# Step sizes of a state-space layer from the plain input, in four column groups of the array

## The chip, the cores and the metric

The kernel runs on one core of a Trainium2 chip. It is a single program in which five engines (PE for matrix products, DVE for elementwise work, ACT for activations and copies, POOL, and SP, which issues the transfers) each follow their own list of instructions and wait for one another through semaphores. The metric is the device time of one execution in microseconds, as the median of several runs.

## The reference: what is computed

One layer of a hybrid decoder is evaluated for a prompt of 1024 tokens and for eight short samples of 4 tokens, together 1056 columns. What matters here is the beginning of the layer:

```python
h = rmsnorm(x, norm_mix)
proj = h @ w_in
z, xbc, dt_raw, v_pool = jnp.split(proj, [D_SSM, D_SSM + D_XBC, D_SSM + D_XBC + SSM_HEADS], axis=-1)
xbc, conv_new = causal_dwconv(conv_buf, xbc, ssm_conv_w, ssm_conv_b)
xbc = jax.nn.silu(xbc)
...
dt = jax.nn.softplus((dt_raw + ssm_dt_bias).astype(f32))
a = -jnp.exp(ssm_a_log.astype(f32))
y, ssm_new = ssd_chunked(xs, dt, a, ...)
```

`dt_raw` is the projection of the normalized input onto 16 columns, one for each head of the recurrence: its step sizes. From them follow the decays, exp of running sums of `dt * a` in chunks of 128 tokens, which the recurrence needs. All is float32.

## The kernel before

Everything lies transposed: 128 channels on the partitions, the 1056 tokens along the free axis, as three blocks of 352 (`NB`, `BW`). The input x is eight such tiles, `xs[0..7]`. To reach float32 accuracy at the fast rate, most products are made in three passes from numbers split into a high and a low part of type float32r: weight high by input high, high by low, low by high. `x_split` makes `hh[k]` and `hl[k]` from `xs[k]` times the gain `norm_mix`. The factor of the norm (one for each token) is not known then; it is applied to the results afterwards, by `normed`, from the tile `rbc`.

**Foreground.** `mm_full` makes one tile of 128 output channels: eight steps over the input tiles, each with 9 matmuls of 352 columns, and after each step one call of `tick()`. The first two tiles are made together by `two_tiles` (16 ticks). A third follows, then the step sizes, then nine more tiles of the convolved part (`XBC_ORDER`), then 16 of gate and pooling (`VZ`), the output product of the pooling half (8 tiles), and the memory's K and V. The tiles' results stand in `pmm`, two buffers of three PSUM banks each, which the tiles take in turn; a tile can begin when the one before the last has been evicted. Two further banks (`mstile`) serve all small products. Weights come in half tiles through three buffers each of raw, high and low parts: ACT writes the high part (`wh`), DVE the low one (`wl`), two halves ahead of their use.

**Ticks.** `later(n, fn)` runs `fn` at the n-th tick from there. `background(gen, every)` puts a generator in a queue and runs a step of its head each `every` ticks. In this queue follow one another: the fold (`fold_pool`, which multiplies two weight matrices, 24 matmuls of 512 columns for each of four groups, 40 yields in all and a 41st call that ends it), the recurrence (`ssd_all`), its sample part (`ssd_sample`) and the gate (`gate_all`, 45 calls, what is left of it being run at the end of the K and V stage). A scheduler orders the instructions of each engine within the bounds of what is declared here; a flag (`strict`) keeps the written order in the beginning of the program.

**The steps that the change touches,** by the lines of the program before:

- `x_sq` (L513), at ticks 8 to 15: ACT squares `xs[k]` in place, DVE adds it into `xs[0]`. `norm_cols` at tick 18 sums over channels by PE transposes and DVE reductions and makes the factors; `x_bc` (L520) at tick 24 spreads them into `rbc` by further PE transposes (`ms<-cst,nr`).
- `dt_weights` (L526) at tick 10: ACT and DVE split the 16 weight columns into high and low, side by side as 32 columns.
- Behind the third tile, the step sizes (L706 to L712): for each of eight input tiles the 32 weight columns against `hh[k]` and `hl[k]`, 48 matmuls of 352 columns in all, into one 3-bank buffer, with a tick after each of the eight. While these run, the fold's first group is put between them. DVE applies the norm's factors (L713, L714).
- `dt_chain` (L534), six ticks later: nine PE transposes bring the step sizes' 32 rows onto token partitions, DVE adds the two halves and the bias, ACT and DVE make softplus by exp and a polynomial, four PE products (with `U`, ones, and two small masks) make the running sums and totals, and ACT makes the decays. The running sums go to DRAM (`scr_acs`), from where the recurrence loads them.

Of the kernel before, what the change touches and what calls it, by code (L numbers as in the profile page):

```python
# [39 lines left out]
SSD_AHEAD = 4  # L40
SAMPLE_EVERY = 1.5
GATE_EVERY = 1.5
FOLD_EVERY = 1.2
WINDOWS = (2, 4, 8, 16)
AHEAD = 2
UP_AHEAD = 5
# [34 lines left out]
def body(ctx, tc, A):  # L81
# [71 lines left out]
    def mmtile():  # L153
        return pmm[0].tile([P, NB, 512], F32, tag="mm", name="mm")
# [220 lines left out]
    def v3(t):  # L375
        return t[:, :T].rearrange("p (b n) -> p b n", b=NB)
# [59 lines left out]
    def bc_cols(r, w, out):  # L436
        c = 0
        while c * P < w:
            ps = mstile()
            c0 = c  # L440
            wsum = 0
            while c < c0 + 4 and c * P < w:
                wc = min(P, w - c * P)
                PE.transpose(ps[:, wsum:wsum + wc], r[:wc, c:c + 1].to_broadcast([wc, P]), ident[:wc, :wc])
                wsum += wc
                c += 1
            V.tensor_copy(out[:, c0 * P:c0 * P + wsum], ps[:, :wsum])
# [63 lines left out]
            prep()  # L511

    def x_sq(k):  # L513
        S.activation(xs[k][:, :T], xs[k][:, :T], AF.Square)
        if k:
            V.tensor_tensor(xs[0][:, :T], xs[0][:, :T], xs[k][:, :T], op=ALU.add)

    xr = []

    def x_bc():  # L520
        xr.append(lp.tile([P, T], F32, tag="rbc", name="rbc", bufs=1))
        bc_cols(xr[0], T, xr[1])

    wd = stile(F32R)[:, :256].rearrange("p (k s h) -> p k s h", k=KT, s=2)

    def dt_weights():  # L526
        wdv = wdr[:, :128].rearrange("p (k h) -> p k h", k=KT)
        S.activation(wd[:, :, 0], wdv, AF.Copy)
        V.tensor_tensor(wd[:, :, 1], wdv, wd[:, :, 0].bitcast(F32), op=ALU.subtract)

    def normed(out, ps):
        V.tensor_tensor(v3(out), ps[:, :, :BW], v3(xr[1]), op=ALU.mult)

    def dt_chain():  # L534
        ps = mstile()
        H2 = 2 * H
        for c in range(8):
            PE.transpose(ps[:, c * H2:(c + 1) * H2], dtr[:H2, c * P:(c + 1) * P], ident[:H2, :H2])
        V.tensor_copy(dtr[:H2, T:T + 2 * TS].rearrange("h (r t) -> h r t", r=2),
                      dtr[:H2, TP:T].unsqueeze(1).to_broadcast([H2, 2, TS]))  # L540
        PE.transpose(ps[:R3, 8 * H2:9 * H2], dtr[:H2, TP:TP + R3], ident[:H2, :H2])
        w = ttile()
        ws = [w[:, i * 144:(i + 1) * 144] for i in range(8)]
        x, u, s, s2, pl, da, ea = ws[:7]

        def v9(a):
            return a.rearrange("p (c h) -> p c h", c=9)

        V.memset(x, 0.0)
        psv = ps[:, :9 * H2].rearrange("p (c s h) -> p c s h", c=9, s=2)  # L550
        dtb = pc("dtb", 0, 16)
        V.tensor_tensor(v9(x)[:, :8], psv[:, :8, 0], dtb.unsqueeze(1).to_broadcast([P, 8, H]), op=ALU.add)
        V.tensor_tensor(v9(x)[:R3, 8], psv[:R3, 8, 0], dtb[:R3], op=ALU.add)
        V.tensor_tensor(v9(x)[:, :8], psv[:, :8, 1], v9(x)[:, :8], op=ALU.add)
        V.tensor_tensor(v9(x)[:R3, 8], psv[:R3, 8, 1], v9(x)[:R3, 8], op=ALU.add)
        V.scalar_tensor_tensor(u, x, -1.0, x, op0=ALU.mult, op1=ALU.min)
        S.activation(u, u, AF.Exp)
        V.tensor_scalar(s, u, 2.0, None, op0=ALU.add)
        V.reciprocal(s, s)
        V.tensor_tensor(s, s, u, op=ALU.mult)  # L560
        V.tensor_tensor(s2, s, s, op=ALU.mult)
        V.tensor_scalar(pl, s2, 1.0 / 15, None, op0=ALU.mult)
        for n in (13, 11, 9, 7, 5, 3):
            V.scalar_tensor_tensor(pl, pl, 1.0 / n, s2, op0=ALU.add, op1=ALU.mult)
        V.scalar_tensor_tensor(pl, pl, 1.0, s, op0=ALU.add, op1=ALU.mult)
        V.tensor_scalar(x, x, 0.0, None, op0=ALU.max)
        dtf = dt_t.rearrange("p c h -> p (c h)")
# [12 lines left out]
        V.tensor_copy(acs_t[:, :8], ps2[:, 0:128].rearrange("p (c h) -> p c h", c=8))  # L580
        V.tensor_copy(acs_t[:R3, 8], ps2[:R3, 256:272])
        V.tensor_tensor(de_t[:, :8], ps2[:, 128:256].rearrange("p (c h) -> p c h", c=8), acs_t[:, :8],
                        op=ALU.subtract)
        V.tensor_tensor(de_t[:R3, 8], ps2[:R3, 272:288], acs_t[:R3, 8], op=ALU.subtract)
        S.activation(cd_t[:, :8], ps2[:, 128:256].rearrange("p (c h) -> p c h", c=8), AF.Exp)
        S.activation(de_t, de_t, AF.Exp)
        V.tensor_tensor(de_t, de_t, dt_t, op=ALU.mult)
        at = ttile()
        for q in range(3):
            ps3 = mstile()  # L590
            n = min(4, 9 - 4 * q)
# [27 lines left out]
    def xbc_raw(f, ps=None):  # L619
        ps = ps or mm_full(KT, hh, hl)  # L620
        raw = ttile()
        if xr[1:]:
            normed(raw[:, 3:3 + T], ps)
        else:
            S.activation(v3(raw[:, 3:3 + T]), ps[:, :, :BW], AF.Copy)
        return raw
# [62 lines left out]
    for k in range(8):  # L689
        later(8 + k, lambda k=k: x_sq(k))  # L690
    later(10, dt_weights)
    later(XN_TICK, lambda: xr.append(norm_cols(xs[0], T, D)))
    later(XN_TICK + XN_LAG, x_bc)
    early_raw = [xbc_raw(f, ps) for f, ps in zip(XBC_ORDER[:2], two_tiles())]
    strict[0] = "after"
    background(fold_pool(), FOLD_EVERY)
    ps = mm_full(KT, hh, hl)
    for f, raw in zip(XBC_ORDER, early_raw):
        V.tensor_tensor(raw[:, 3:3 + T], raw[:, 3:3 + T], xr[1][:, :T], op=ALU.mult)
        xbc_conv(f, raw)  # L700
    raw = ttile()
    normed(raw[:, 3:3 + T], ps)
    xbc_conv(XBC_ORDER[2], raw)

    ps = mmtile()
    for k in range(KT):  # L706
        for pi, x in enumerate((hh[k], hl[k])):
            for b in range(NB):
                PE.matmul(ps[:2 * H, b, :BW], lhsT=wd[:, k].rearrange("p s h -> p (s h)"),
                          rhs=x[:, b * BW:(b + 1) * BW], start=(k == 0 and pi == 0), stop=(k == KT - 1 and pi == 1))  # L710
        tick()
    dtr = ttile()  # L712
    V.tensor_tensor(v3(dtr)[:2 * H], ps[:2 * H, :, :BW], v3(xr[1])[:2 * H], op=ALU.mult)  # L713
    later(6, dt_chain)  # L714
    strict[0] = False
    for f in XBC_ORDER[3:6]:
        xbc_tile(f)
# [217 lines left out]
    def pool_tile(f):  # L935
# [2 lines left out]
        G.memset(raw[:, 0:15], 0.0)  # L938
        ext = raw[:, 1039:1191].rearrange("p (b t) -> p b t", b=8)
        dma(ext[:, :, 0:15], A["pool_hist"][f])  # L940
        rb = v3(xr[1])
        V.tensor_tensor(raw[:, 15:719].rearrange("p (b n) -> p b n", b=2), ps[:, 0:2, :BW], rb[:, 0:2], op=ALU.mult)
        V.tensor_tensor(raw[:, 719:1039], ps[:, 2, :320], rb[:, 2, :320], op=ALU.mult)
        V.tensor_tensor(ext[:, :, 15:19], ps[:, 2, 320:352].rearrange("p (b t) -> p b t", b=8),
# [1081 lines left out]
```

## Time and profile before

| What | Value |
|---|---|
| median of three runs | 1649.13 us (1647.32 to 1649.66) |
| the profiled execution | 1645.04 us |
| its span, first to last instruction | 1642.9 us |
| PE, weight loads, DVE, ACT busy | 1624.7, 1553.6, 1214.1, 806.9 us |
| granted TensorE clock, mean | 0.999 |
| mean busy share of the DMA engines, 36 to 60 us | 0.25 |

All operations of the program go through one helper, so every row names line 93; they are told apart by tiles. `mm` is a 3-bank buffer, `ms` a small PSUM buffer, `s`, `t` and `ld` are working tiles of the kernel, `wh` and `wl` the split weights. In the rows, `mm<-s 128*32 128x352` is a matmul with 128 rows and 32 columns of weights, which streams 352 columns. Matmuls overlap in the records (one of 352 columns is shown with 0.32 us, and the next begins 0.16 after it), so their cost is read from start to start.

### The profile page before, as it was taken

To read this page: it belongs to the slowest core of one execution; us is meant where nothing else is said; L and a number is where in the kernel's file an instruction comes from. 1 tells how busy PE (TensorE), PEld (TensorE's weight loads), DVE (VectorE), ACT (ScalarE), POOL (GpSimd) and SP (SyncE) were. 2 spreads that over 40 slices of the span, in tenths; PEclk is the share of its full clock that TensorE was granted. 3 is DMA by queue.
4 is the path that set the end of the run, shared out by engine and by line. 5 is a ranking of instruction groups with operands and counts; after the bars stand their busy time and mean duration, and the time that the engine had idled before them with its cause. 6 is when DMAs were issued, how large, how long until landed. Compare 5 with 4: busy or idle time off the path is not lost.

```text
span 1642.9 us, 30318 instructions
## 1 busy us (share of the span) xinstructions
PE 1624.7 (99%) x11802; PEld 1553.6 (95%) x11802; DVE 1214.1 (74%) x2044; ACT 806.9 (49%) x1580; POOL 54.2 (3%) x117
## 2 busy tenths in 40 slices
PE   9999999999999999999999999999999999999998
PEld 8899999999989999999888999999999999999997
DVE  7766787788679676654654898888888998766665
ACT  7566643543505343223543665666665556554441
POOL 0110000001000000000000000000000000000000
PEclk9999999999999999999999999999999999999999
DMA  6244354544687688953755654544344356985542
GB/s 224 86 156 97 69 112 105 117 90 118 220 304 253 210 271 296 301 184 91 253 199 189 220 179 133 163 133 144 108 126 159 120 174 208 315 287 181 167 131 106
DMA packets 172286, 287.40 MB, mean 175 GB/s; under 512 B 39680, under 2 KB 77408, under 8 KB 172144
## 3 DMA queue, kind: packets, MB, share of 16 engines
q1 hardware_dynamic: 169280, 281.02, 54.3%
q0 software_dynamic: 2864, 4.46, 1.9%
q8 instruction: 92, 1.51, 0.4%
q14 instruction: 50, 0.41, 0.1%
HBM read 207.89 MB, written 77.53 MB: 174 GB/s over the span
## 4 chain that ended last, share of the span: by engine, by line
PE 89%; DMA 5%; DVE 4%; ACT 1%; issue 1%; SPq 0%; ACTq 0%; DVEq 0%
PE mb L93 60%; PE mm L93 22%; PE ms L93 6%; DVE s L93 2%; DMA q<-scr_g 2%; DVE wl L93 1%; ACT s L93 1%; DMA ld<-scr_pool 1%; DVE t L93 0%; DMA s<-xT 0%; SPq L93 0%; DMA ld<-scr_acs 0%; DMA t<-scr_z 0%; DMA ld<-h0T 0%; DMA wr<-scr_dn 0%
## 5 line engine op out<-in xcount | busy, mean ns | idle before, releaser
L93 PE MATMUL mb<-s,wh 128*128 128x264 f32 (+4 forms) x4800 | 901.5, 294 | 2.9 <-ACT wh L93 2.9
L93 PEld LDWEIGHTS mb<-s,wh 128*128 128x128 f32 x4800 | 756.6, 188 | 9.2 <-ACT wh L93 3.6
L93 PE MATMUL mb<-s,wl 128*128 128x264 f32 (+4 forms) x2400 | 663.4, 294 | 2.4 <-DVE wl L93 2.4
L93 PEld LDWEIGHTS mb<-s,wl 128*128 128x128 f32 x2400 | 445.0, 188 | 7.2 <-DVE wl L93 4.3
L93 ACT ACTIVATE wh<-wr 128x512 fp32r<-128x512 f32 (+1 forms) x266 | 164.2, 618 | 365.6 <-PE mb L93 170.1
L93 PE MATMUL mm<-s,wh 128*128 128x352 f32 x1728 | 340.3, 330 | 2.3 <-ACT s L93 1.3
L93 PEld LDWEIGHTS mm<-s,wh 128*128 128x128 f32 x1728 | 284.6, 188 | 8.5 <-ACT s L93 2.7
L93 DVE TENSOR_TENSOR wl<-wr,wh 128x512 fp32r<-128x512 f32 (+1 forms) x266 | 178.8, 673 | 103.0 <-ACT wh L93 101.4
L93 PE MATMUL mm<-s,wl 128*128 128x352 f32 x864 | 187.4, 323 | 0.0
L93 DVE SCALAR_TENSOR_TENSOR t<-t,par 128x1104 f32<-128x1104 f32 (+1 forms) x124 | 168.6, 1364 | 18.1 <-ACT t L93 17.3
L93 PEld LDWEIGHTS mm<-s,wl 128*128 128x128 f32 x864 | 147.2, 189 | 1.7 <-issue 1.2
L93 DVE TENSOR_TENSOR t<-t 128x1024 f32<-128x1024 f32 (+10 forms) x147 | 105.4, 729 | 8.2 <-DMA t<-w_dn 4.9
L93 ACT ACTIVATE wh<-ws 128x512 fp32r<-128x512 f32 x110 | 69.0, 628 | 71.0 <-PE mb L93 69.0
L93 DVE TENSOR_TENSOR wl<-ws,wh 128x512 fp32r<-128x512 f32 x110 | 75.6, 687 | 22.5 <-ACT wh L93 17.0
L93 DVE TENSOR_TENSOR s<-mb,s 128x264 f32<-128x264 f32 (+6 forms) x140 | 60.9, 472 | 30.3 <-PE mb L93 15.1
L93 ACT ACTIVATE t<-mb 128x264 f32<-128x264 f32 (+1 forms) x136 | 53.5, 394 | 57.9 <-PE mb L93 51.0
L93 ACT ACTIVATE s<-s 128x512 f32<-128x512 f32 (+7 forms) x87 | 65.1, 764 | 31.4 <-DMA s<-scr_acs 21.7
L93 DVE TENSOR_TENSOR s<-q,s 128x528 fp32r<-128x528 f32 x81 | 56.1, 703 | 24.3 <-ACT s L93 24.0
L93 ACT ACTIVATE t<-t,par 128x1104 f32<-128x1104 f32 (+1 forms) x56 | 73.0, 1304 | 1.5 <-DVE t L93 0.6
L93 ACT ACTIVATE s<-q 128x528 fp32r<-128x528 f32 x81 | 51.7, 643 | 41.2 <-DMA q<-scr_g 39.1
L93 DVE TENSOR_TENSOR s<-s 128x528 fp32r<-128x528 f32 (+8 forms) x76 | 64.5, 867 | 6.8 <-ACT s L93 6.3
L93 PE MATMUL mb<-s 128*128 128x256 f32 (+2 forms) x414 | 68.9, 323 | 0.0
(202 smaller groups left out, 1496.5 us busy)
## 6 DMA issues: line engine op xcount, KB each, us to landing
q<-scr_g SPq DMA_DIRECT2D x77, 264.0 KB, 3.7
wr<-w_up SPq DMA_DIRECT2D x59, 256.0 KB, 2.9
wr<-w_in SPq DMA_DIRECT2D x56, 256.0 KB, 3.2
wr<-w_mo SPq DMA_DIRECT2D x46, 256.0 KB, 2.8
scr_g<-t SPq DMA_DIRECT2D x22, 528.0 KB, 2.7
ws<-w_up SPq DMA_DIRECT2D x44, 256.0 KB, 2.9
t<-w_dn SPq DMA_DIRECT2D x32, 256.0 KB, 4.3
scr_dn<-t SPq DMA_DIRECT2D x32, 256.0 KB, 2.9
```

The source lines that it names most:

```text
L93: i = fn(*args, **kwargs)
```

## The change

1. The step sizes are made from plain x, not from the split input. The weight columns are multiplied by the gain `norm_mix` (DVE) and padded with zeros from 16 to 32 columns. Input tiles k = 0 to 3, and then 4 to 7, go to the four groups of 32 output partitions of one buffer: each group sums two of the eight input tiles. These are 24 plain float32 matmuls of 352 columns. They stand between the first two tiles and the third, without ticks. ACT copies the result, 128 rows, out of PSUM.
2. x must stay until then, so the squares go to other tiles and their sum to a tile of its own.
3. `dt_chain` applies the norm's factors, and instead of transposing multiplies each 128 tokens (as the weights) by `sel`, a 128 by 16 matrix of zeros and ones that adds up the four groups (the padded columns meet no one). These are nine plain float32 matmuls with 16 moving columns. Two of DVE's four additions behind them go.
4. The fold's steps come each 1.05 ticks instead of 1.2, and `dt_chain` ten ticks after the third tile, instead of six after the old place of the step sizes.

```diff
-FOLD_EVERY = 1.2
+FOLD_EVERY = 1.05
...
     def x_sq(k):
-        S.activation(xs[k][:, :T], xs[k][:, :T], AF.Square)
-        if k:
-            V.tensor_tensor(xs[0][:, :T], xs[0][:, :T], xs[k][:, :T], op=ALU.add)
+        if k == 0:
+            xr.append(stile())
+            S.activation(xr[0][:, :T], xs[0][:, :T], AF.Square)
+        else:
+            t = ttile()
+            S.activation(t[:, :T], xs[k][:, :T], AF.Square)
+            V.tensor_tensor(xr[0][:, :T], xr[0][:, :T], t[:, :T], op=ALU.add)
...
-    wd = stile(F32R)[:, :256].rearrange("p (k s h) -> p k s h", k=KT, s=2)
+    wd = stile()[:, :256].rearrange("p (k h) -> p k h", k=KT)
+    sel = xa.tile([P, H], F32, name="sel")
+    dtr3 = xa.tile([P, R3], F32, name="dtr3")
+    dtr = stile()
 
     def dt_weights():
-        wdv = wdr[:, :128].rearrange("p (k h) -> p k h", k=KT)
-        S.activation(wd[:, :, 0], wdv, AF.Copy)
-        V.tensor_tensor(wd[:, :, 1], wdv, wd[:, :, 0].bitcast(F32), op=ALU.subtract)
+        V.memset(wd, 0.0)
+        V.tensor_tensor(wd[:, :, :H], wdr[:, :128].rearrange("p (k h) -> p k h", k=KT),
+                        pc("norm_mix", 0, 8).unsqueeze(2).to_broadcast([P, KT, H]), op=ALU.mult)
+        V.tensor_reduce(sel, ident.rearrange("p (i h) -> p h i", h=H), axis=AX.X, op=ALU.add)
+
+    def dt_raw():
+        ps = mmtile()
+        for k in range(0, KT, 4):
+            for b in range(NB):
+                for j in range(4):
+                    PE.matmul(ps[32 * j:32 * j + 32, b, :BW], lhsT=wd[:, k + j],
+                              rhs=xs[k + j][:, b * BW:(b + 1) * BW], start=(k == 0), stop=(k == 4))
+        S.activation(v3(dtr), ps[:, :, :BW], AF.Copy)
...
     def dt_chain():
+        V.tensor_tensor(dtr[:, :T], dtr[:, :T], xr[2][:, :T], op=ALU.mult)
+        V.tensor_copy(dtr3.rearrange("h (r t) -> h r t", r=3), dtr[:, TP:T].unsqueeze(1).to_broadcast([P, 3, TS]))
         ps = mstile()
-        H2 = 2 * H
-        for c in range(8):
-            PE.transpose(ps[:, c * H2:(c + 1) * H2], dtr[:H2, c * P:(c + 1) * P], ident[:H2, :H2])
-        V.tensor_copy(dtr[:H2, T:T + 2 * TS].rearrange("h (r t) -> h r t", r=2),
-                      dtr[:H2, TP:T].unsqueeze(1).to_broadcast([H2, 2, TS]))
-        PE.transpose(ps[:R3, 8 * H2:9 * H2], dtr[:H2, TP:TP + R3], ident[:H2, :H2])
+        for c in range(9):
+            x = dtr[:, c * P:(c + 1) * P] if c < 8 else dtr3
+            PE.matmul(ps[:P if c < 8 else R3, c * H:(c + 1) * H], lhsT=x, rhs=sel, start=True, stop=True)
...
     early_raw = [xbc_raw(f, ps) for f, ps in zip(XBC_ORDER[:2], two_tiles())]
+    dt_raw()
     strict[0] = "after"
     background(fold_pool(), FOLD_EVERY)
     ps = mm_full(KT, hh, hl)
...
-    ps = mmtile()
-    for k in range(KT):
-        for pi, x in enumerate((hh[k], hl[k])):
-            for b in range(NB):
-                PE.matmul(ps[:2 * H, b, :BW], lhsT=wd[:, k].rearrange("p s h -> p (s h)"),
-                          rhs=x[:, b * BW:(b + 1) * BW], start=(k == 0 and pi == 0), stop=(k == KT - 1 and pi == 1))
-        tick()
-    dtr = ttile()
-    V.tensor_tensor(v3(dtr)[:2 * H], ps[:2 * H, :, :BW], v3(xr[1])[:2 * H], op=ALU.mult)
-    later(6, dt_chain)
+    later(10, dt_chain)
```

More of the change, by code (lines that the diff above doesn't have):

```diff
@@ L521, in x_bc @@
         xr.append(lp.tile([P, T], F32, tag="rbc", name="rbc", bufs=1))
-        bc_cols(xr[0], T, xr[1])
-    wd = stile(F32R)[:, :256].rearrange("p (k s h) -> p k s h", k=KT, s=2)
-    def dt_weights():
-        wdv = wdr[:, :128].rearrange("p (k h) -> p k h", k=KT)
-        S.activation(wd[:, :, 0], wdv, AF.Copy)
-        V.tensor_tensor(wd[:, :, 1], wdv, wd[:, :, 0].bitcast(F32), op=ALU.subtract)
+        bc_cols(xr[1], T, xr[2])
+    wd = stile()[:, :256].rearrange("p (k h) -> p k h", k=KT)
+    sel = xa.tile([P, H], F32, name="sel")
+    dtr3 = xa.tile([P, R3], F32, name="dtr3")
+    dtr = stile()
+    def dt_weights():
+        V.memset(wd, 0.0)
[10 more added lines that the diff above has]
+        S.activation(v3(dtr), ps[:, :, :BW], AF.Copy)
     def normed(out, ps):
-        V.tensor_tensor(v3(out), ps[:, :, :BW], v3(xr[1]), op=ALU.mult)
+        V.tensor_tensor(v3(out), ps[:, :, :BW], v3(xr[2]), op=ALU.mult)
     def dt_chain():
+        V.tensor_tensor(dtr[:, :T], dtr[:, :T], xr[2][:, :T], op=ALU.mult)
+        V.tensor_copy(dtr3.rearrange("h (r t) -> h r t", r=3), dtr[:, TP:T].unsqueeze(1).to_broadcast([P, 3, TS]))
         ps = mstile()
-        H2 = 2 * H
-        for c in range(8):
-            PE.transpose(ps[:, c * H2:(c + 1) * H2], dtr[:H2, c * P:(c + 1) * P], ident[:H2, :H2])
-        V.tensor_copy(dtr[:H2, T:T + 2 * TS].rearrange("h (r t) -> h r t", r=2),
-                      dtr[:H2, TP:T].unsqueeze(1).to_broadcast([H2, 2, TS]))
-        PE.transpose(ps[:R3, 8 * H2:9 * H2], dtr[:H2, TP:TP + R3], ident[:H2, :H2])
+        for c in range(9):
+            x = dtr[:, c * P:(c + 1) * P] if c < 8 else dtr3
+            PE.matmul(ps[:P if c < 8 else R3, c * H:(c + 1) * H], lhsT=x, rhs=sel, start=True, stop=True)
         w = ttile()
@@ L549, in dt_chain @@
         V.memset(x, 0.0)
-        psv = ps[:, :9 * H2].rearrange("p (c s h) -> p c s h", c=9, s=2)
+        psv = ps[:, :9 * H].rearrange("p (c h) -> p c h", c=9)
         dtb = pc("dtb", 0, 16)
[L552 to L555, printed above, removed]
+        V.tensor_tensor(v9(x)[:, :8], psv[:, :8], dtb.unsqueeze(1).to_broadcast([P, 8, H]), op=ALU.add)
+        V.tensor_tensor(v9(x)[:R3, 8], psv[:R3, 8], dtb[:R3], op=ALU.add)
         V.scalar_tensor_tensor(u, x, -1.0, x, op0=ALU.mult, op1=ALU.min)
@@ L621, in xbc_raw @@
         raw = ttile()
-        if xr[1:]:
+        if xr[2:]:
             normed(raw[:, 3:3 + T], ps)
@@ L691, in body @@
     later(10, dt_weights)
-    later(XN_TICK, lambda: xr.append(norm_cols(xs[0], T, D)))
+    later(XN_TICK, lambda: xr.append(norm_cols(xr[0], T, D)))
     later(XN_TICK + XN_LAG, x_bc)
     early_raw = [xbc_raw(f, ps) for f, ps in zip(XBC_ORDER[:2], two_tiles())]
+    dt_raw()
     strict[0] = "after"
@@ L698, in body @@
     for f, raw in zip(XBC_ORDER, early_raw):
-        V.tensor_tensor(raw[:, 3:3 + T], raw[:, 3:3 + T], xr[1][:, :T], op=ALU.mult)
+        V.tensor_tensor(raw[:, 3:3 + T], raw[:, 3:3 + T], xr[2][:, :T], op=ALU.mult)
         xbc_conv(f, raw)
@@ L940, in pool_tile @@
         dma(ext[:, :, 0:15], A["pool_hist"][f])
-        rb = v3(xr[1])
+        rb = v3(xr[2])
         V.tensor_tensor(raw[:, 15:719].rearrange("p (b n) -> p b n", b=2), ps[:, 0:2, :BW], rb[:, 0:2], op=ALU.mult)
```

## The prediction

> **What bounds the kernel now.** I read the page first, then the waits, then the order of time on the engine that carries the span.
>
> ```profile
> span 1642.9 us, 30318 instructions
> PE 1624.7 (99%) x11802; PEld 1553.6 (95%) x11802; DVE 1214.1 (74%) x2044; ACT 806.9 (49%) x1580; POOL 54.2 (3%) x117
> ```
>
> The reader should see that TensorE is without work for only 18 us of the span. The stages that the change touches lie between 30 and 600 us. The list of waits, narrowed to 36 to 600 us and to PE, has three rows (who waited for whom: us in total, times, longest):
>
> ```profile
> PE ms L93 <- DVE xd L93: 0.7, 1, 0.7
> PE ms L93 <- issue: 0.4, 1, 0.4
> PE mm L93 <- DVE s L93: 0.3, 1, 0.3
> ```
>
> That is 1.4 us in 564. So what PE no longer does there comes off the end, every wait that the change adds goes on it, and no more than 1.4 us of old waits can be won back. The profiled execution took 1645.04 us, 2.14 more than its span, and 4.1 less than the median of the three runs (1649.13). I count the difference in the profiled execution and take it off the median. A difference under 0.2% (3.3 us) counts as none, since the three runs alone lie 2.3 us apart.
>
> **What goes from PE.** The timeline of PE, from the broadcast of the norm on (start, us, operation, output<-input, rows*columns, moving size, count):
>
> ```profile
> 45.94 1.05 PE L93 MATMUL mm<-s 128*32 128x352 f32 x5
> 46.92 0.24 PE L93 MATMUL ms<-cst,nr 32*128 32x32 f32 x1
> 47.09 0.67 PE L93 MATMUL mm<-s 128*32 128x352 f32 x3
> 47.61 1.62 PE L93 MATMUL ms<-s 128*128 128x512 f32 x6
> 49.07 0.80 PE L93 MATMUL mm<-s 128*32 128x352 f32 x4
> 49.70 1.55 PE L93 MATMUL ms<-s 128*128 128x512 f32 x6
> 51.09 1.13 PE L93 MATMUL mm<-s 128*32 128x352 f32 x6
> 52.06 1.54 PE L93 MATMUL ms<-s 128*128 128x512 f32 x6
> 53.44 1.11 PE L93 MATMUL mm<-s 128*32 128x352 f32 x6
> 54.39 1.53 PE L93 MATMUL ms<-s 128*128 128x512 f32 x6
> 55.76 3.98 PE L93 MATMUL mm<-s 128*32 128x352 f32 x24
> 59.58 1.13 PE L93 MATMUL mm<-s,wh 128*128 128x352 f32 x6
> ```
>
> Durations overlap, so I count from start to start. The 48 step-size matmuls (mm<-s, 32 columns) hold 0.98 + 0.52 + 0.63 + 0.97 + 0.95 + 3.82 = 7.87 us; the 24 in between (ms<-s) are the fold and stay. The nine transposes of the old step sizes stand in a later row:
>
> ```profile
> 71.85 0.73 PE L93 MATMUL ms<-cst,t 32*128 32x32 f32 x9
> 72.51 0.91 PE L93 MATMUL mm<-s,wh 128*128 128x352 f32 x4
> ```
>
> They hold 0.66. In all 8.53 us go.
>
> **What comes: the 24 plain matmuls.** A plain f32 matmul is two passes in the trace (the kernel's three warm-up matmuls, first row below, count six), so 24 make 48 passes, in 12 sets of four, one for each column group of the array. Before has no such block at 352 columns, but the sample attention has one at 256, four column groups with different moving tiles:
>
> ```profile
> 1.49 4.76 PE L93 MATMUL ms<-warm 128*128 128x512 f32 x6 [1.49 <-DVE dtp L93]
> ...
> 831.92 1.12 PE L93 MATMUL mb<-s 128*128 128x256 f32 x8
> 832.98 1.07 PE L93 MATMUL mb<-t,pm 128*32 128x256 f32 x16
> 833.86 1.05 PE L93 MATMUL mb<-ld,pm 128*32 128x256 f32 x16
> 834.84 1.09 PE L93 MATMUL mb<-cst,p 128*128 128x128 f32 x8
> ```
>
> Sixteen passes, four sets, take 0.88 us from start to start: 0.22 a set, so the four groups run together. The second sixteen, followed by full-width work, take 0.98: leaving the narrow form costs 0.10. Scaled by columns (352/256) a set is 0.30, twelve are 3.6, and with 0.1 on either side 3.8 us. The dearest row for such passes, from the groups of the whole run, is that of the recurrence's sample part, in bursts of eight:
>
> ```profile
> L93 PE MATMUL ms<-ld,s 128*32 128x256 f32 x64 | 6.9, 391 | 0.1
> ```
>
> It is 0.108 a pass, 0.148 at 352 columns, 7.1 us for 48. I take 3.8, because the burst here is long and without a break, as in the sixteens; 3.6 and 7.1 are the ends.
>
> On packing, the Trainium skill ("TensorE: Matmul & The Clock Gate", Part 3) gives a measured speed-up of 3.07 for four tiles, not four, and "TensorEngine Tiling (Array Packing)", Key Properties, says that changing the tiling mode drains the array. By 3.07 the block would be 4.6 us (48 passes one by one at 0.30, divided), 0.8 more than I take, and the sum below would be -1.3. The trace agrees with a cost of leaving (the 0.10 above), and shows the full factor inside a burst.
>
> The order shows the block in one piece on PE, ahead of the third tile (s is input, w and h in wh and wl the split weights):
>
> ```order
>  L93 MATMUL mm<-s,wh 128x352 x6
>  L93 MATMUL mm<-s,wl 128x352 x3
> +L93 MATMUL mm<-s 32x352 x24
>  L93 MATMUL mm<-s,wh 128x352 x6
>  L93 MATMUL mm<-s,wl 128x352 x3
> ```
>
> It begins as soon as the second tile is done, into the banks that the first left. And at the old place, behind the broadcast of the norm (ms<-cst,nr), the fourth tile takes over the room between the fold's matmuls:
>
> ```order
>  L93 MATMUL ms<-cst,nr 128x128 x8
> -L93 MATMUL mm<-s 32x352 x5
> +L93 MATMUL mm<-s,wh 128x352 x5
>  L93 MATMUL ms<-cst,nr 128x32
> -L93 MATMUL mm<-s 32x352 x3
> +L93 MATMUL mm<-s,wh 128x352
> +L93 MATMUL mm<-s,wl 128x352 x2
>  L93 MATMUL ms<-s 128x512 x6
> -L93 MATMUL mm<-s 32x352 x4
> +L93 MATMUL mm<-s,wl 128x352
>  L93 MATMUL ms<-s 128x512 x6
> ```
>
> The fold still finds foreground work to stand between, so nothing of it is bared.
>
> **The selecting matmuls.** Nine products with a 128-column weight and 16 moving columns, 18 passes. Nearest are the decay products, of the same plain kind (eight passes, the PE wait of 0.4 just before them):
>
> ```profile
> 83.94 1.12 PE L93 MATMUL ms<-t,cst 128*128 128x128 f32 x8 [0.37 <-issue]
> 84.99 0.43 PE L93 MATMUL mm<-s,wl 128*128 128x352 f32 x1
> ```
>
> 1.05 us for eight is 0.131 a pass, with two beginnings in it; the old transposes were 0.073. So 18 cost between 1.3 and 2.4, and I take 2.1, nearer to the like kind.
>
> **The wait at the decays.** On DVE the chain that makes the decays is cut by weight splits (wl), which wait for PE to free a buffer. Before, at its end (t and dtp are the chain):
>
> ```order
> L93 TENSOR_TENSOR wl_1004<-wr_883,wh_1002 128x512
> L93 TENSOR_SCALAR t_760<-t_760 128x144
> L93 SCALAR_TENSOR_TENSOR t_760<-t_760 128x144 x7
> L93 SCALAR_TENSOR_TENSOR dtp_94<-t_760 128x144
> L93 TENSOR_TENSOR t_760<-dtp_94,t_760 128x144
> ```
>
> Now:
>
> ```order
> L93 TENSOR_TENSOR wl_1032<-wr_903,wh_1030 128x512
> L93 TENSOR_TENSOR t_800<-t_800 128x144 x2
> L93 TENSOR_SCALAR t_800<-t_800 128x144
> L93 SCALAR_TENSOR_TENSOR t_800<-t_800 128x144 x7
> L93 TENSOR_TENSOR wl_1127<-wr_979,wh_1125 128x512
> L93 SCALAR_TENSOR_TENSOR dtp_94<-t_800 128x144
> L93 TENSOR_TENSOR t_800<-dtp_94,t_800 128x144
> ```
>
> A split has moved behind the polynomial. Its buffer comes free with the fourth of the eight steps of the sixth tile, and PE meets the decay products one step and a matmul later. The timing of the same pieces before, on ACT and DVE:
>
> ```profile
> 78.93 0.63 ACT L93 ACTIVATE wh<-wr 128x512 fp32r<-128x512 f32 x1 [0.96 <-PE mm L93]
> 78.00 0.23 DVE L93 TENSOR_SCALAR t<-t 128x144 f32<-128x144 f32 x1 [2.46 <-ACT t L93]
> 79.92 0.68 DVE L93 TENSOR_TENSOR wl<-wr,wh 128x512 fp32r<-128x512 f32 x1
> 80.52 0.23 DVE L93 TENSOR_SCALAR t<-t 128x144 f32<-128x144 f32 x1
> 83.19 0.31 DVE L93 SCALAR_TENSOR_TENSOR dtp<-t 128x144 f32<-128x144 f32 x1
> 83.53 0.31 DVE L93 TENSOR_TENSOR t<-dtp,t 128x144 f32<-128x144 f32 x1
> ```
>
> From the freed buffer to the chain's end it was 4.91 us (78.93 to 83.84); without the part that now stands ahead (80.52 to 83.19, 2.67) it is 2.2. PE arrives about 1.4 after the buffer came free: a step of 1.45 and a matmul of 0.16, less the 0.2 that the last results take to land (estimates from the timeline). So it waits some 0.9 where it waited 0.37: +0.5. Behind PE's wait only its own tile is queued; DVE's next evictions wait with it, with the fold's 24 matmuls (18 before) as cover.
>
> **What costs nothing.** ACT now copies the new block out of PSUM, behind the second tile's eviction:
>
> ```profile
> 32.64 1.06 ACT L93 ACTIVATE t<-mm 128x1056 f32<-128x1056 f32 x1 [1.32 <-PE mm L93]
> 46.18 1.38 DVE L93 COPY rbc<-ms 128x512 f32<-128x512 f32 x3
> 57.67 1.25 DVE L93 TENSOR_TENSOR t<-mm,rbc 128x1056 f32<-128x1056 f32 x1
> ```
>
> The third tile needs the second's banks (free at 33.70); the 3.8 us of the new block, from about 32.5 (just before that copy could begin), hide that, and an uncovered eviction would cost 1.06. The third tile's own eviction ended at 58.92, 0.66 before PE took its banks at 59.58. It now has the scaling of the step sizes (about 1.2) ahead of it, but its banks are wanted only by the fifth tile, after a tile of 8 steps and the fold: some 4 us of cover instead. The squares go to other tiles at the same length; the weights' scaling and the selecting sum on DVE lie between them, and the new block gives DVE 3.8 us more before the norm's transposes. Without it, under 1 us. The SP queue issues the same loads, w_in's two units ahead; POOL's small copies follow the tiles as before.
>
> The fold has 41 calls: at 1.2 ticks it ended in tick 50, ten ticks into the tiles after the sixth; with eight ticks fewer and 1.05 it ends in tick 44, twelve into them. So recurrence, sample and gate run two ticks (2.9 us) later against the foreground, in the same pattern. This can bite where the gate's last group is wanted, at the end of the K and V stage (DVE's last split, PE's first and eighth step of the next tile):
>
> ```profile
> 593.59 2.44 DVE L93 TENSOR_TENSOR s<-s 128x1056 fp32r<-128x1056 f32 x2
> 592.00 1.13 PE L93 MATMUL mb<-s,wh 128*128 128x352 f32 x6
> 602.18 1.13 PE L93 MATMUL mb<-s,wh 128*128 128x352 f32 x6
> ```
>
> Ready at 596.0, wanted at 602.2: 6.2 us of cover, 3.3 after the shift. Nothing, then; beyond that, each us late is a us. The eight steps also give the 1.45 a step used above (10.18 / 7).
>
> **The sum.** -8.53 + 3.8 + 2.1 + 0.5 = -2.1 us. The profiled execution would take 1642.9, the median 1647.0.
>
> **Rivals.**
>
> *Faster by more than 0.2%.* The wait at 83.94 does not come back (-0.9), the other old waits go as the recurrence meets other moments of the tiles (-1.0), and the selecting passes cost what the transposes did (-0.8): -4.8, 1644.3. For it: 0.073 is a row of this kernel, and waits so small are chance. Against it: all must go well, and a shift makes new waits as easily. Part of it is enough: -3.3 needs 1.2 of these 2.7. Chance 0.32.
>
> *Slower: the decay chain comes late.* Its place is the decay products in the sixth tile. If ACT's exponential or the split before the polynomial comes behind a further silu or eviction, DVE's chain slips, and PE stands for all of the slip. It decides beyond 5.4 us of slip (2.1 + 3.3). At 6.2, two weight splits and three convolution steps, the time is 4.1 longer, 1653.2. For it: DVE had waited 2.46 us for that exponential at 78.00 already, and the chain stands before the fifth tile's eviction. Against it: PE's program has no other chain there, and I count DVE ahead of PE by a few us when the polynomial starts. Chance 0.08.
>
> *Slower: the column groups do not overlap* at 352 columns. Then 48 passes at 0.30 are 14.4, with the sides 14.6, 10.8 more than taken: +8.7, 1657.8. The sixteens speak against it. Chance 0.04.
>
> *The change does not do what it says*: the order shows the block where the diff puts it, so this is left out.
>
> **How the numbers follow.** The forecast has 0.56, and I predict 1647.0. Its own ends are the block at 7.1 (+3.3: 1650.3) and, below, the selecting passes and the wait at their best (1645.3). The range reaches down to the faster rival less the spread of the runs, 1643.0, and up to 1650.5; it leaves out the slower rivals, 0.12. Faster 0.32, same 0.56, slower 0.12.
>
> **What would show it.** In the profile after: 48 passes mm<-s 128*32 in one piece from about 32.5 us, lasting 3.6 to 4 from their start to the next tile; no such rows between the fold's; 18 passes with sel in 1.3 to 2.4 us; an idle stretch of 0.5 to 1.3 before ms<-t,cst, some 8 us into the sixth tile; no wait of PE near 600. I am wrong if the block lasts over 5 us, if PE's waits between 36 and 600 pass 3 us, or if the step of the sum that fails is one that I put at nothing.

## The result, and the profile after

The changed kernel takes 1671.15 us (median of four runs, 1668.77 to 1672.28) where the kernel before, in the same series, takes 1648.22 (1645.44 to 1649.66). The ratio is 1.0142, 95% interval 1.0128 to 1.0156: 23 us slower. The prediction was 1647.0.

The head of the page after; the profiled execution took 1668.77 us:

```profile
span 1666.3 us, 30335 instructions
PE 1629.2 (98%) x11811; PEld 1555.4 (93%) x11811; DVE 1213.3 (73%) x2044; ACT 797.3 (48%) x1574; POOL 58.8 (4%) x117
```

TensorE stands for 37.1 us of this span, where it stood for 18.2. Before looking for the rest, the priced parts, in the timeline of PE:

```profile
32.21 3.76 PE L93 MATMUL mm<-s 128*32 128x352 f32 x48
35.90 1.24 PE L93 MATMUL mm<-s,wh 128*128 128x352 f32 x6
...
69.94 1.85 PE L93 MATMUL ms<-sel,s 128*128 128x16 f32 x16
71.64 0.32 PE L93 MATMUL ms<-sel,dtr 128*96 128x16 f32 x2
71.81 1.21 PE L93 MATMUL mm<-s,wh 128*128 128x352 f32 x6
...
88.16 1.15 PE L93 MATMUL ms<-t,cst 128*128 128x128 f32 x8
```

The block of 48 passes lasts 3.69 us from start to start, the 18 selecting passes 1.87, and the decay products find their data there: the last row shows no idle time. So none of the loss is in these priced parts. The list of PE's waits between 36 and 600 us, which before held 1.4 us, says where it is:

```profile
PE ms L93 <- DVE cbm L93: 7.1, 3, 3.4
PE ms L93 <- DVE s L93: 5.8, 2, 3.4
PE ms L93 <- DVE xd L93: 5.0, 5, 1.4
```

`cbm`, `xd` and `s` are tiles of the recurrence (`ssd_group`, `ssd_pre`, `ssd_post`). DVE makes them from the two small PSUM banks `ms`, and PE cannot reuse a bank before DVE has read it. All of these waits lie between 200 and 410 us. One row for that stretch, before and then after (length, busy PE, weight loads, DVE, ACT, POOL, granted clock, DMA share, GB/s):

```profile
200.00:410.00 210.00, 209.34 (x1541) 195.89 (x1540) 165.47 (x353) 84.05 (x154) 5.68 (x19) 1.00 0.49 108
```

```profile
200.00:410.00 210.00, 190.95 (x1358) 176.28 (x1357) 145.09 (x318) 76.75 (x145) 0.66 (x6) 0.98 0.46 97
```

PE stands for 19.05 us instead of 0.66, and its clock is lower. DVE is less busy than before, too: it is not overloaded, it is waiting. The row of its waits that grows most is the one for ACT's work on `s` tiles (this stretch, before, then after: us in total, times, longest):

```profile
DVE s L93 <- ACT s L93: 1.8, 2, 1.6
```

```profile
DVE s L93 <- ACT s L93: 15.6, 6, 4.5
```

ACT's waits, in turn, begin at the loads of the running sums (before, then after):

```profile
ACT ld L93 <- DMA ld<-scr_acs: 44.4, 11, 4.9
ACT s L93 <- DMA s<-scr_acs: 21.7, 10, 3.5
```

```profile
ACT s L93 <- DMA s<-scr_acs: 55.0, 9, 9.6
ACT ld L93 <- DMA ld<-scr_acs: 32.2, 10, 4.4
ACT s L93 <- DVE s L93: 24.6, 9, 9.5
```

ACT waited for these loads before the change as well, 66 us in all, and it cost nothing. After the change the same two waits come to 87 us, and PE stands.

**How one stall is built.** The recurrence has 32 units, alternately in `s` and in `ld` tiles, and three tiles of either kind hold their loads. In the kernel before, a load is issued as soon as the unit three of its kind before has been multiplied, and PE wants its result three pairs of units later. There the sixth `s` load is issued at 203.50, and the sixth block of products with an `s` tile begins at 249.20 (SyncE's timeline, then PE's):

```profile
203.50 0.36 SPq L93 DMA_DIRECT2D s<-scr_acs  x1
```

```profile
249.20 0.44 PE L93 MATMUL ms<-s,xd 128*64 128x128 f32 x4
```

Those are 45.7 us. ACT and DVE, however, begin on the tile at once, in an order that was fixed when the program was built. After the change, on SyncE, ACT, DVE and PE in turn:

```profile
204.17 0.61 SPq L93 DMA_DIRECT2D o_pool_s<-t  x1
204.88 0.62 SPq L93 DMA_DIRECT2D s<-scr_acs  x1
...
216.16 0.33 SPq L93 DMA_DIRECT2D wr<-w_in  x1
216.58 0.39 SPq L93 DMA_DIRECT2D ld<-scr_acs  x1
```

```profile
213.57 0.63 ACT L93 ACTIVATE s<-s 128x512 f32<-128x512 f32 x1 [7.36 <-DMA s<-scr_acs]
...
221.28 0.63 ACT L93 ACTIVATE ld<-ld 128x512 f32<-128x512 f32 x1 [3.64 <-DMA ld<-scr_acs]
```

```profile
214.24 0.69 DVE L93 TENSOR_TENSOR s<-s 128x512 f32<-128x512 f32 x1 [4.54 <-ACT s L93]
214.85 0.68 DVE L93 TENSOR_TENSOR xd<-ms,dtp 128x512 f32<-128x512 f32 x1
215.45 0.68 DVE L93 TENSOR_TENSOR wl<-wr,wh 128x512 fp32r<-128x512 f32 x1
...
221.95 0.69 DVE L93 TENSOR_TENSOR ld<-ld,s 128x512 f32<-128x512 f32 x1 [3.85 <-ACT ld L93]
222.56 0.68 DVE L93 TENSOR_TENSOR xd<-ms,dtp 128x512 f32<-128x512 f32 x1
```

```profile
223.29 0.33 PE L93 MATMUL ms<-cst,s 128*128 128x128 f32 x1 [1.25 <-DVE xd L93]
...
228.95 0.66 PE L93 MATMUL ms<-cst,s 128*128 128x128 f32 x2 [2.20 <-DVE cbm L93]
```

Read it from the bottom. PE waits at 223.29 for `xd` (222.56), which frees a bank. Ahead of that `xd` on DVE stands a multiplication of a fresh `ld` tile, which waited 3.85 us for ACT, and ACT 3.64 for the load. That load was issued at 216.58, behind a load of `w_in`, whose buffer the split at 215.45 had to free; and that split stood behind another multiplication of a fresh tile (214.24, waited 4.54). Work that PE wants some 45 us after its load holds up work that PE wants now, and through SyncE's queue it also holds up the next load.

The cause could be the two ticks by which the change shifts the recurrence against the tiles (theory A, with several forms), or something that the change computes or holds (rival B).

### The profile page after: what moved, and what is told of

It is laid out like the page before. It is cut to its first block, busy times and chain, and to the rows that moved or that the text cites. A ratio compares the mean times of both kernels' runs of the same rounds, so it can differ in the third digit from the quotient of the medians.

```text
span 1666.3 us, 30335 instructions
## 1 busy us (share of the span) xinstructions
PE 1629.2 (98%) x11811; PEld 1555.4 (93%) x11811; DVE 1213.3 (73%) x2044; ACT 797.3 (48%) x1574; POOL 58.8 (4%) x117
## 4 chain that ended last, share of the span: by engine, by line
PE 69%; DMA 7%; DVE 6%; ACT 2%; issue 1%; SPq 0%; DVEq 0%; ACTq 0%
PE mb L93 57%; PE mm L93 9%; PE ms L93 3%; DVE t L93 2%; DVE s L93 2%; DMA q<-scr_g 2%; DMA ld<-scr_acs 2%; DMA s<-scr_acs 1%; DVE wl L93 1%; ACT s L93 1%; DMA ld<-scr_pool 1%; SPq L93 0%; DMA t<-scr_z 0%; ACT ld L93 0%; DVE xd L93 0%
## 5 line engine op out<-in xcount | busy, mean ns | idle before, releaser
L93 ACT ACTIVATE s<-s 128x512 f32<-128x512 f32 (+7 forms) x79 | 58.0, 744 | 89.6 <-DMA s<-scr_acs 55.0
L93 DVE TENSOR_TENSOR s<-s 128x528 fp32r<-128x528 f32 (+6 forms) x68 | 55.7, 836 | 21.0 <-ACT s L93 21.0
```

Source lines behind the costliest of these rows:

```text
L93: i = fn(*args, **kwargs)
```

## The experiments

**Only the shift, taken from the change (e1).**

```diff
-FOLD_EVERY = 1.05
+FOLD_EVERY = 1.02
```

> The changed kernel with its fold steps at 1.02 ticks: the fold ends in tick 42, ten ticks into the tiles behind the sixth, as in the kernel before; everything else of the change stays. Theory A (the loss is the recurrence's shift of two ticks against the tiles): the 23 us are gone, 1646 us in a series where the kernel before has 1648, ratio 0.998 to 1.000, PE without work for under 2 us between 200 and 410. Rival B (the loss comes from what the change computes or holds, whatever the shift): still about 1671, ratio 1.012 to 1.016.

Measured 1646.01 us, ratio 0.9975 (0.9965 to 0.9986). PE between 200 and 410:

```profile
200.00:410.00 210.00, 208.53 (x1532) 195.07 (x1531) 164.12 (x354) 81.55 (x150) 5.55 (x18) 1.00 0.49 108
```

The loss is gone, all of it, with every other part of the change in place. It is a little below the band that A gave.

**Only the shift, given to the kernel before (e2).**

```diff
-FOLD_EVERY = 1.2
+FOLD_EVERY = 1.25
```

> The kernel before, with its fold steps at 1.25 ticks: the fold ends in tick 52, twelve ticks into the tiles behind the sixth, as in the changed kernel; nothing else of the change is in it. Theory A: it loses as the changed kernel does, 1668 to 1674 us, ratio 1.012 to 1.016, PE without work for 15 to 25 us between 200 and 410. Rival B: 1647 to 1650, ratio within 0.002 of 1.

Measured 1679.31 us, ratio 1.0184 (1.0163 to 1.0205), with PE standing for 23.3 us in that stretch:

```profile
200.00:410.00 210.00, 186.72 (x1309) 171.95 (x1308) 143.24 (x318) 74.16 (x142) 0.77 (x7) 0.98 0.47 93
```

B falls: nothing of the change is in this kernel, and it loses more than the changed one. A holds; the size is 5 us over the band that it gave.

**SyncE's queue (e3).** The recurrence's loads go to GpSimd's queue, at 1.05.

```diff
-        dma(at[:, 0:512].rearrange("p (h l) -> p h l", h=4),
+        G.dma_start(at[:, 0:512].rearrange("p (h l) -> p h l", h=4),
```

> The changed kernel, fold steps at 1.05, in which the recurrence's 32 loads of scr_acs are issued by GpSimd instead of SyncE, so that they no longer stand behind stores and loads of w_in in SyncE's order. Theory Q (a form of A: the shift costs because SyncE's queue holds the recurrence's loads back): most of the 23 us are gone, 1646 to 1653 us, ratio under 1.004. Rival D (the shift costs by the order of DVE's and PE's own work, and the queue matters little): 1662 us or more, ratio over 1.008.

Measured 1661.26 us, ratio 1.0062 (1.0046 to 1.0077): between the two bands. About half of the loss goes with the queue, and neither theory has it whole. The loads still took a while to land (issues in the stretch, of e3 and then of the changed kernel; KB each, median us to landing):

```profile
s<-scr_acs POOLq DMA_DIRECT2D x11, 256.0 KB, 7.3
ld<-scr_acs POOLq DMA_DIRECT2D x11, 256.0 KB, 5.6
```

```profile
s<-scr_acs SPq DMA_DIRECT2D x11, 256.0 KB, 8.3
ld<-scr_acs SPq DMA_DIRECT2D x11, 256.0 KB, 5.1
```

**Another shift (e4).**

```diff
-FOLD_EVERY = 1.05
+FOLD_EVERY = 1.2
```

> The changed kernel with its fold steps at 1.2 ticks, the number of the kernel before: the fold ends in tick 50, eighteen ticks in. In SyncE's order the recurrence's odd loads then stand behind the pool tile's o_pool stores and its even ones behind the scr_pool store. Theory Q: it loses too, 8 us or more over e1 (1655 us or more). Rival A alone, read as a matter of the two ticks only: no statement of size. Rival B: about 1671, as with 1.05.

Measured 1684.16 us, ratio 1.0205 (1.0188 to 1.0222). The number is the one that theory Q asked for, but its reason is not there. PE, SyncE, ACT, DVE and PE again, in one stall of e4:

```profile
225.57 0.44 PE L93 MATMUL ms<-ld,xd 128*64 128x128 f32 x4
```

```profile
226.71 0.38 SPq L93 DMA_DIRECT2D ld<-scr_acs  x1
```

```profile
235.04 0.63 ACT L93 ACTIVATE ld<-ld 128x512 f32<-128x512 f32 x1 [11.27 <-DMA ld<-scr_acs]
```

```profile
235.70 0.69 DVE L93 TENSOR_TENSOR ld<-ld,s 128x512 f32<-128x512 f32 x1 [5.08 <-ACT ld L93]
...
238.20 0.69 DVE L93 TENSOR_TENSOR wl<-wr,wh 128x512 fp32r<-128x512 f32 x1 [1.80 <-ACT wh L93]
```

```profile
240.22 0.41 PE L93 MATMUL ms<-cst,s 128*128 128x128 f32 x2 [2.04 <-DVE s L93]
```

The load leaves 1.14 us after the products that free its tile have begun, as promptly as in the kernel before (210.34 to 211.48 there). The other loads do the same: the median load leaves 0.3 us after the last product of its tile with `xd` has ended, in e4 as in the kernel before, where it is 1.9 us in the changed kernel (22 loads in each trace, from the sixth of either kind on). The 8.3 us from this load to the start of the exponential are enough: ACT's next instruction in order needs it, and everything behind waits. Q as the whole cause falls here. That left the loads' latency (theory L) against the bare order of the instructions (rival D).

**No loads (e5).** At 1.05, GpSimd sets the tiles instead.

```diff
-        dma(at[:, 0:512].rearrange("p (h l) -> p h l", h=4),
-            scr["acs"][h0:h0 + 4, c * P:(c + 1) * P].partition_broadcast(P))
+        G.memset(at[:, 0:512], -1.0)
```

> The changed kernel, fold steps at 1.05, with the recurrence's 32 loads left out: GpSimd sets the same tiles to -1 instead (the decays are left out of the recurrence's result, every later operation is kept). No load stands in a queue and none has a latency. Theory L (the shift costs because the loads come just in time, and their landing is then on a loop through ACT, DVE and PE): the loss is gone, under 1652 us, PE without work for under 4 us between 200 and 410. Rival D (the order of DVE's own instructions at this shift is enough): 1657 us or more, as with the loads on GpSimd's queue (1661).

Measured 1645.95 us, ratio 0.9975 (0.9962 to 0.9988), and PE does not stand at all:

```profile
200.00:410.00 210.00, 210.00 (x1544) 196.90 (x1543) 164.79 (x348) 83.07 (x148) 17.05 (x41) 1.00 0.33 82
```

The shift without the loads costs nothing. Every later operation is kept, and DVE's order is the bad one still (the table under e9), so D falls: the order hurts only through the latency of what it waits for.

**The control for e3 (e6).** The diff of e1 and that of e3 together.

> The changed kernel with fold steps at 1.02 (e1), with the 32 loads issued by GpSimd. It is the control for e3: if GpSimd's queue costs something of its own, it costs it here too. Theory Q with no cost of the queue itself: as e1, 1645 to 1649 us. If the 11.6 us that were left in e3 belong to GpSimd's queue: 1654 us or more.

Measured 1643.88 us, ratio 0.9962 (0.9948 to 0.9976). GpSimd's queue has no cost of its own here, so what e3 left belongs to the shift.

**Two more shifts (e7 and e8).** `FOLD_EVERY` at 1.04 and at 1.0.

> The changed kernel with fold steps at 1.04: the fold ends in tick 43, eleven ticks in, one tick later than in e1 and one earlier than in the changed kernel. In SyncE's order the recurrence's even loads stand ahead of the pool tile's stores in most tiles and between them in some. Theory Q: between the two, nearer to e1: 1646 to 1655 us. Theory A, read as a cost in proportion to the shift: about 1658.

> The changed kernel with fold steps at 1.0: the fold ends in tick 41, nine ticks in. In SyncE's order the even loads stand ahead of the stores in every pool tile. Theory Q: as e1 or better, 1643 to 1649 us. If only ten ticks in are good: 1652 us or more.

Measured 1642.32 us for e7, ratio 0.9957 (0.9943 to 0.9971), with no idle time of PE between 200 and 410, and 1651.75 us for e8, ratio 1.0015 (1.0002 to 1.0027). So the cost is not in proportion to the shift: one tick costs nothing, two cost 23 us. e7 is better than any theory had it. e8 lies between its two bands; PE stands for only 1.4 us between 200 and 410 there, as in e1 (1.5). Its profile has 5.8 us more of standing than that of e1 (25.7 against 19.9); 2.7 of these lie in the first 100 us, and the rest is spread over the later stages. What causes them was not tested.

The tick in which the fold ends is not yet the shift that counts. The recurrence's steps come each 3 ticks at first and each 1.6 only in the tiles of gate and pooling. Counted in the traces by the foreground's matmuls that stand ahead of each block of products with an `s` tile, the blocks from the third to the sixteenth follow one another every 8 steps of the foreground (in e4 some after 7 or 9). Against the kernel before they come 0 steps later in e1 and e8, 1 in e7, 2 in the changed kernel and in e2, and 5 or 6 in e4. So e8 meets the tiles as e1 does, and e4, whose fold ends eight ticks after that of e1, is not a whole round behind it.

**Later use, same shift (e9).** If an early wait on a fresh load is what hurts, then it must be enough to put the first use later on ACT and DVE. `done` holds the last state update of each unit; the added dependence only orders instructions and makes no new wait for data.

```diff
+    done = []
...
+        first = []
         if c > 0:
-            S.activation(ce, am, AF.Exp)
+            first.append(S.activation(ce, am, AF.Exp))
...
-                S.activation(am[:, i], am[:, i], AF.Relu, scale=-1.0, bias=a)
+                first.append(S.activation(am[:, i], am[:, i], AF.Relu, scale=-1.0, bias=a))
...
-                V.tensor_scalar(am[:, i], am[:, i], a, 0.0, op0=ALU.subtract, op1=ALU.min)
+                first.append(V.tensor_scalar(am[:, i], am[:, i], a, 0.0, op0=ALU.subtract, op1=ALU.min))
+        for i in first if done else ():
+            tc.add_manual_dep(i.ins, done[-1], NOSYNC, reason="order")
...
-            V.tensor_tensor(hs, hs, pst, op=ALU.add)
+            done.append(V.tensor_tensor(hs, hs, pst, op=ALU.add).ins.name)
```

> The changed kernel, fold steps at 1.05, loads on SyncE as they were; only the order of the recurrence's own work on ACT and DVE changes: the first operations that read a fresh load (its exponential, its subtraction) are kept behind the state update of the unit two before, where the scheduler had put them up to four units earlier. Theory H (head of the line: an instruction that waits for a fresh load, whose result PE wants only some 45 us later, stands on DVE and ACT ahead of work that PE wants now): the loss is gone, under 1651 us, PE without work for under 4 us between 200 and 410. If instead the queue of SyncE is what costs (theory Q): the loads still stand behind the same stores, and it stays above 1660.

Measured 1644.05 us, ratio 0.9986 (0.9973 to 1.0000). The loads are on SyncE's queue, the shift is that of the changed kernel, and the loss is gone:

```profile
200.00:410.00 210.00, 210.00 (x1543) 196.86 (x1541) 169.32 (x359) 86.73 (x160) 5.10 (x18) 1.00 0.51 109
```

DVE now waits for PE, as it should (its two largest waits in the stretch follow; the wait for ACT's `ld`, 27.6 us in the changed kernel, is not in the list any more), and ACT waits for no `scr_acs` load at all:

```profile
DVE xd L93 <- PE ms L93: 15.0, 13, 1.6
DVE s L93 <- PE ms L93: 11.5, 28, 1.2
```

SyncE's order in this stretch is that of the changed kernel, but for a few neighbours that have changed places (mostly loads of `w_in`), and the `s` loads still stand behind the `o_pool` stores; yet the median load leaves 0.3 us after the last product of its tile with `xd`. PE's order between 60 and 460 us is that of the changed kernel, too, but for two places that differ by a matmul or two. So neither queue order nor PE's order costs anything by itself here.

The trace also shows what the shift had done to the order. Counted on DVE, in the second half of the recurrence (units 18 to 31, for which 18 to 31 `xd` products belong ahead): so many `xd` products stand ahead of the first seven multiplications by a fresh tile's exponential.

| Kernel | `xd` ahead (18, 19, 20, 21, 22, 23, 24 would be their own place) | us |
|---|---|---|
| before, and e1, alike | 16, 16, 16, 17, 20, 20, 21 | 1648 to 1650, 1646 |
| changed, e2 and e5, alike | 15, 15, 16, 17, 19, 20, 20 | 1671, 1679, 1646 (no loads) |
| e7 | 15, 16, 16, 18, 20, 20, 21 | 1642 |
| e4 | 14, 16, 16, 18, 18, 20, 20 | 1684 |
| e9 | 17, 19, 20, 21, 22, 23, 24 | 1644 |

In the kernel before these were already two to four units early. The change put four of the seven one unit earlier still, and e4 some of them two; the edit puts nearly all in their own place. e5 has the changed kernel's list without its loss, since nothing is waited for. e7 is near the list of before, though not in each entry: the list shows the direction, and where exactly the edge lies it does not show.

**The same edit at other shifts (e10, e11), and on the kernel before (e12).**

> The same edit on e4 (fold steps at 1.2, the worst shift so far, 1684 us, in which the loads were not held back by SyncE's queue). Theory H: under 1652 us. If the shift costs through PE's own order, which stays: above 1670.

> The same edit on e7 (fold steps at 1.04, the best so far, 1642.3 us). Theory H: little is left to win, within 3 us of e7; the waits of PE between 200 and 410 fall under 1 us.

> The kernel before (step sizes as they were, fold steps at 1.2) with the edit of e9 on ACT's and DVE's order and nothing else. Theory H: before has no wait to win back (0.7 us between 200 and 410), so it stays within 0.2%: ratio 0.998 to 1.002; what e9 to e11 have over it is then the worth of the change itself, 2 to 4 us. If the edit brings something of its own: ratio under 0.998.

| Kernel | Median us | Ratio to before, 95% |
|---|---|---|
| e10: e4 with the edit | 1646.32 | 0.9999 (0.9989 to 1.0008) |
| e11: e7 with the edit | 1641.12 | 0.9971 (0.9961 to 0.9981) |
| e12: before with the edit | 1647.99 | 0.9994 (0.9980 to 1.0008) |

In e10 the edit takes e4 from 2% slower to no difference, at a shift that it does not touch, and with PE's order between 63 and 460 us that of e4. In e12 it brings nothing of its own, as theory H said; the other half of that expectation, that e9 to e11 lie 2 to 4 us under it, came true for e11 alone (see the next section). In e11 there was little left to win: its interval and that of e7 overlap. Theory H stands: a first use put too early, times the latency of the load, with SyncE's queue adding about half in the changed kernel, where the entries ahead of the loads are late themselves. Why a shift of two steps puts the first uses where they hurt, and one of one step does not, was not taken apart further.

e7 and e11 are faster than the kernel before, by 0.4% and 0.3%, and faster than the changed one.

## Why the prediction was wrong

**The sum was nearly right.** It had the block at 3.8 us (measured 3.69), the selecting passes at 2.1 (1.87), and a wait at the decays that grows by 0.5. That wait vanished instead: 0.37 less, the one term with the wrong sign. By the rows, -8.53 + 3.69 + 1.87 - 0.37 is -3.3 us where I had -2.1. e1, in which the recurrence has the order it had before, measures 0.9975 of the kernel before: 4.1 us less, interval 2.3 to 5.8. With the edit of e9 the worth hangs on the fold's steps: against e12's 0.9994 the ratios of e9, e10 and e11 are 0.0008 lower, 0.0005 higher and 0.0023 lower, which is 1.3 us less, 0.8 more and 3.8 less, each uncertain by about 3 us (from the intervals of the two ratios). So the runs agree with a gain of a few microseconds but do not measure it closely. Two small sums do not come out, and nothing hangs on them: 14.4 divided by 3.07 is 4.7, not 4.6, and the faster rival less the runs' spread of 2.3 is 1642.0, not 1643.0.

**The column groups** run side by side throughout the long burst. The price taken from the sample attention's sixteens held. One pass alone would take about 0.30 us, an estimate from the records of the decay products in the kernel before, whose passes of 128 columns begin 0.111 us apart; 48 of these are 14.4 us, and 3.69 us is a factor of 3.9. The factor of 3.07 in the Trainium skill ("TensorE: Matmul & The Clock Gate", Part 3) was measured for four row tiles with 512 moving columns; by it the block would be an estimated 4.7 us. For the four column groups here the trace does not agree, and the measurement decides.

**The step that failed** is in the part on what costs nothing: "So recurrence, sample and gate run two ticks (2.9 us) later against the foreground, in the same pattern." I asked what a shift costs only at its far end, where the gate's last group is wanted. The recurrence's own 32 units lay in between, and I passed over them. Five steps of 1.6 ticks make a pair of units, and these 8 ticks are exactly one tile of the foreground. So a shift does not average out: 14 of the 16 pairs meet a tile at the same place in it, and PE's waits come eleven times between 200 and 410 us, 19 us in all. "In the same pattern" was wrong, too: on DVE the first uses of fresh loads stood up to a unit earlier among the recurrence's work, and what waited behind them was wanted by PE at once. With it failed "The SP queue issues the same loads, w_in's two units ahead". They were the same loads, in another order: the recurrence's stood behind stores and `w_in` (204.88, 216.58).

**What misled me** was a view that is true but one-sided. PE's waits, 1.4 us in 564, bound what can be won. They say nothing of how near the other engines are to making it wait. The rows that do say it were in the same trace: ACT's 66 us of waiting for `scr_acs` loads, and on DVE, between 200 and 410,

```profile
DVE ld L93 <- ACT ld L93: 20.3, 8, 4.2
```

An engine that waits for a load 4.2 us at a time, with PE's next need behind that instruction, has no cover that can be counted on. Such a row says where a loss can come from, not that there is one. In e1, where PE hardly stands, it is longer still:

```profile
DVE ld L93 <- ACT ld L93: 26.4, 8, 4.5
```

I read off a cover of 6.2 us near 600 and took it for the stage.

**The rivals.** The slower rival had the right kind of mechanism, a chain on DVE that comes late, at the wrong place: the decays (88.16) were on time. The column groups that do not overlap were refuted by the 3.69 us. What I named as a sign of being wrong, waits of PE over 3 us between 36 and 600 and a failing step among those put at nothing, is what came: the three rows above hold 17.9 us.

## What to carry to other kernels

A background whose period equals the foreground's has a phase, and a change that adds or drops a few steps ahead of it moves that phase for all of its rounds: try two or three phases before judging the change itself. Where an engine's fixed order holds instructions that wait for a fresh load, look at what stands behind them and not at who waits now; putting the first use later, nearer to where it is wanted, made three shifts out of three safe here (e9, e10 and e11: 1644.05, 1646.32 and 1641.12 us where the kernel before took 1646.56). A list of the bottleneck's waits bounds the gain of a change and never its loss.

## What the runs showed of the hardware that was not expected

The standing cost more than its own time. From e1's profile to the changed kernel's, PE's idle time grows by 17.2 us (19.9 to 37.1) and its busy time by 5.6 (1623.6 to 1629.2), though the work is the same. The windows around two of the stalls of the changed kernel show where that comes from (clock in the third column from the right):

```profile
224.00:229.00 5.00, 2.80 (x19) 2.51 (x17) 5.00 (x14) 0.42 (x2) 0.11 (x1) 1.00 0.22 17
229.00:233.00 4.00, 4.00 (x25) 3.62 (x27) 1.43 (x3) 0.00 (x0) 0.00 (x0) 0.57 0.47 58
```

```profile
264.00:268.00 4.00, 0.83 (x6) 0.53 (x4) 4.00 (x9) 0.63 (x1) 0.11 (x1) 1.00 0.32 20
268.00:272.00 4.00, 3.73 (x32) 3.28 (x33) 3.03 (x8) 0.00 (x0) 0.00 (x0) 1.00 0.59 95
```

After PE had stood for 2.20 us in the first, the granted clock over the next 4 us was 0.57; after 3.45 us in the second (264.83 to 268.27) it stayed at 1.00. So the length of a stall does not decide. The trace of the changed kernel has three slow stretches, from 229.02, 389.44 and 580.59 us, each 3.41 us long at a granted clock of 0.50. Half of their length is lost, 5.1 us in all, which is most of the 5.6. Their starts lie 160.42 and 191.15 us apart, 47 and 56 times 3.413 us, so they fit one grid of windows that runs on whatever the program does. On this grid the stall of 2.20 us lies within one window, the one just ahead of the slow stretch at 229.02. The stall of 3.45 us is cut by a window's edge into 1.74 and 1.70. Ahead of the other two slow stretches PE stood for 2.52 and 1.75 us of the window. In these windows it is PE's standing within one that counts, and the edge lies near half of its length; 1.74 without a slow stretch and 1.75 with one do not place it more closely, as the ends of matmuls in the records are modelled.

The Trainium skill ("TensorE: Matmul & The Clock Gate", Part 1) has a gate that passes half of the pulses after an idle window of about 3.4 us, in windows that run freely. The trace agrees on the length and on the free run. It does not agree that the window must be idle throughout: 2.20 us of 3.41 were enough.

That the issuing engine mattered was not expected either. The Trainium skill ("DMA: Bandwidth & Descriptors", Issuing engines are not separate DMA queues) says that issuing from several engines only saves the time that issuing takes, usually small beside the transfer. At the shift of the changed kernel the runs do not agree: in e3 it was worth 10 us (1671.15 to 1661.26; 13 by the ratios of the two series, 1.0142 and 1.0062), because a queue that waits in order for one entry holds the next ones too: the load at 216.58 left only after the load of `w_in` at 216.16, and that one only when its buffer was free. At the shift of e1 there was little to win (e1 0.9975, e6 0.9962, intervals that overlap).
